# A hybrid encoder layer: the recurrent mixer's output products reordered, and 64-row passes padded with zero rows

## The chip, the cores and the metric

The kernel runs on one core of one Trainium2 chip. The metric is the device time of one execution, in microseconds (us), as the median of three runs. Engines are called by their names in the profile: PE (TensorE, matrix products; PEld is its loading of weights), DVE (VectorE), ACT (ScalarE), POOL (GpSimd) and SP (which issues DMAs). A matrix product writes to PSUM, which the other engines then read.

## What is computed

One layer over 1024 frames of width 1024: a half-step feed-forward network (FFN) with layer norm, a mixer, and a second half-step FFN. The mixer projects the frames once and feeds two branches, a recurrent one with 8 heads of 64 (RWKV-7) and a latent attention; both are gated, summed and projected.

```python
def layer(h):
    h = layer_norm(ALPHA * h + 0.5 * swiglu(h, ffn1_w1, ffn1_w3, ffn1_w2), ln1_g, ln1_b)
    proj = h @ w_in
    p_shift, p_mla, gate_logits = split(proj)
    y_rwkv = rwkv7_mixer(p_shift, ...) @ w_up_rwkv
    y_mla = mla_mixer(p_mla, ...) @ w_up_mla
    mix = (g_rwkv * y_rwkv + g_mla * y_mla) @ w_o
    h = layer_norm(ALPHA * h + mix, ln2_g, ln2_b)
    return layer_norm(ALPHA * h + 0.5 * swiglu(h, ffn2_w1, ffn2_w3, ffn2_w2), ln3_g, ln3_b)

def rwkv7_mixer(...):          # per head: a 64 x 64 state that every frame decays and updates
    w = -softplus(-(w0 + tanh(wd) @ w_decay_up)) - 0.5
    a = sigmoid(a0 + ad @ w_iclr_up)
    state = state * w_t + sa * b_t + v_t * k_t      # scan over the frames
    y_t = state @ r_t
```

## The kernel before, in words

**Precision.** A float32 operand is split into a rounded part (`hi`) and the rest (`lo`), and a product is three matrix passes, hi·hi, hi·lo and lo·hi (`mm3`, lines 273 to 275). The last FFN tile is only 64 wide: `ffn_stage1` puts its `hi` into rows 0 to 63 of `gh` and its `lo` into rows 64 to 127 (lines 325 to 327), against weights that the host stacked twice. So one pass over 128 rows gives hi·hi and lo·hi (line 356), and a second pass over rows 0 to 63 alone gives hi·lo (line 357). `lora_za` (lines 587 and 588), the two low-rank products with inner width 64 (for `w0` and `a0`), works in the same manner.

**FFN.** `block` runs over groups of tiles of the hidden width. Each of the two FFNs has one group (the last, tiles 18 to 21) that holds the 64-wide tile: for 8 row tiles and 2 halves it issues three `mm3` and the pair of lines 356 and 357, 11 matmuls in all. `load_w` brings a weight tile in: a DMA, the rounding on ACT (line 218) and the rest on POOL (line 219).

**Mixer.** PE's order is written out by hand here (`mid` turns the scheduler off for PE alone). The recurrent branch is four tasks of two heads each (`rwkv_task`). Between its steps a task yields a number, and `drive` fills PE for about so many microseconds with other work: jobs of `Fill`, mostly `dense` projections of three 128-row matmuls a step. Each job's weights are loaded up to two jobs ahead. At the end of a task, a chain over 16 chunks of 64 frames gives the states `sa` (lines 870 to 876), and the output products follow (lines 878 to 888): for each head `hd` of the pair and each chunk c a product with `m` and `qv` (128 rows, line 884), and for c > 0 one with `rr` and the state (the 64 rows of that head, line 887), which is added to the first. Chunk c writes PSUM rows 0 to 63 or 64 to 127 after its parity. A task thus issues 62 products, and each is two instructions in the trace: 124. One head fills one PSUM tile of the pool `pr`, which has three, and ACT copies each out to `y` (line 888). Then DVE, ACT and POOL normalize `y` (lines 894 to 902), while PE does 11 us of filling (`GAP["gn"]`), and PE transposes the result (line 909). Behind the mark "gn" the next task's features begin; behind the fourth task the attention's first loads do.

The tile scheduler sets the order on DVE, ACT, POOL and SP, and PE's outside the mixer.

Of the kernel before, what the change touches and what calls it, by code (L numbers as in the profile page):

```python
# [9 lines left out]
F32 = mybir.dt.float32  # L10
F32R = mybir.dt.float32r
AF = mybir.ActivationFunctionType
ALU = mybir.AluOpType
# [3 lines left out]
P = 128  # L17
# [4 lines left out]
HALF = 512  # L22
D_FF = 2752
NF = D_FF // P
# [3 lines left out]
NCH = S // CH  # L28
# [179 lines left out]
    return K.wsp if K.wsp2 is None or K.wn % 2 else K.wsp2  # L208


def load_w(K, src, n=1024, rows=P):
    nc = K.nc
    raw = K.wraw.tile([P, 1024], F32, name="raw")
    (nc.gpsimd if K.pq else nc.sync).dma_start(out=raw[:rows, :n], in_=src)
    pool = w_pool(K)
    hi = pool.tile([P, 1024], F32R, name="wh", tag="w")
    lo = pool.tile([P, 1024], F32R, name="wl", tag="w")
    nc.scalar.copy(out=hi[:rows, :n], in_=raw[:rows, :n])  # L218
    nc.gpsimd.tensor_tensor(out=lo[:rows, :n], in0=raw[:rows, :n], in1=hi[:rows, :n].bitcast(F32), op=ALU.subtract)  # L219
    return hi, lo  # L220

# [109 lines left out]
def block(K, stage1, w2, groups, ln, resid, emit_h, last=False):  # L331
    nc = K.nc
    accs = [None] * NT
    hT = None
    for gi, fs in enumerate(groups):
        gs = [stage1(f) for f in fs]
        first, final = gi == 0, gi == len(groups) - 1
        ws = [load_w(K, w2[f]) for f in fs]
        if final:
            gb = ln_begin(K, ln)  # L340
        for t in range(NT):
            tsl = slice(t * P, (t + 1) * P)
            if first:
                accs[t] = K.acc.tile([P, D], F32, name="acc", tag="acc")
                r = K.tmp.tile([P, D], F32, name="r", tag="r", bufs=2)
                nc.sync.dma_start(out=r, in_=resid(t))
            for n, ns in halves():
                ps = K.py.tile([P, HALF], F32, name="y", tag="y")
                for q in range(len(fs)):
                    gh, gl = gs[q]  # L350
                    wh, wl = ws[q]
                    st, sp = q == 0, q == len(fs) - 1
                    if gl is not None:
                        mm3(nc, ps, gh[:, tsl], gl[:, tsl], wh[:, ns], wl[:, ns], st, sp)
                    else:
                        nc.tensor.matmul(ps, lhsT=gh[:, tsl], rhs=wh[:, ns], start=st, stop=False)
                        nc.tensor.matmul(ps, lhsT=gh[0:64, tsl], rhs=wl[0:64, ns], start=False, stop=sp)
                if first:
                    nc.vector.scalar_tensor_tensor(out=accs[t][:, ns], in0=r[:, ns], scalar=ALPHA, in1=ps,  # L359
                                                   op0=ALU.mult, op1=ALU.add)  # L360
                elif final:
                    if n == 0:
                        su = K.small.tile([P, 2], F32, name="su")
                    nc.vector.scalar_tensor_tensor(out=accs[t][:, ns], in0=accs[t][:, ns], scalar=1.0, in1=ps,
                                                   op0=ALU.mult, op1=ALU.add, accum_out=su[:, n:n + 1])
                else:
                    nc.vector.tensor_tensor(out=accs[t][:, ns], in0=accs[t][:, ns], in1=ps, op=ALU.add)  # L367
            if final:
                hT = ln_tile(K, t, accs[t], su, gb, hT, emit_h, transpose=not last)
    return hT  # L370
# [183 lines left out]
def prt(K, name="pr"):  # L554
    return K.pr.tile([P, HALF], F32, name=name, tag="pr")


def load_w2(K, src, n=HALF, rows=P):
    nc = K.nc
    raw = K.wraw.tile([P, 1024], F32, name="raw")  # L560
    (nc.gpsimd if K.pq else nc.sync).dma_start(out=raw[:rows, :n], in_=src)
    w = w_pool(K).tile([P, 2, HALF], F32R, name="w2", tag="w")
    nc.scalar.copy(out=w[:rows, 0, :n], in_=raw[:rows, :n])
    nc.gpsimd.tensor_tensor(out=w[:rows, 1, :n], in0=raw[:rows, :n], in1=w[:rows, 0, :n].bitcast(F32), op=ALU.subtract)
    return w


# [9 lines left out]
            return  # L577


def lora_za(K, x, n, rows, bias, w):  # L580
    nc = K.nc
    for i in range(NRT):
        csl = slice(i * P, (i + 1) * P)
        o = K.d.tile([P, S], F32, name="lo", tag="d")
        for h, hs in halves():
            ps = prt(K)
            nc.tensor.matmul(ps, lhsT=w[:, 0, csl], rhs=x[:, hs], start=True, stop=False)
            nc.tensor.matmul(ps, lhsT=w[rows, 1, csl], rhs=x[rows, hs], start=False, stop=True)
            nc.scalar.activation(out=o[:, hs], in_=ps, func=AF.Sigmoid, bias=vec(K, bias, i))
            yield 0.43  # L590
        nc.sync.dma_start(out=K.lod[i, n], in_=o)
# [95 lines left out]
def rwkv_task(K, i, r, k, v, store):  # L687
    nc = K.nc
    yield from rwkv_features(K, i, r, k, v)
    ar, bk, yb, wl = K.feat  # L690
    yield GAP["bk"]
    hd_ = lambda h: slice(h * 64, h * 64 + 64)

    bkt, qv, pq = [], [], []
    for h in range(2):
        bt = rt(K, "bkt", [P, 8, P])
        for b in range(2):
            ps = prt(K)
            for q in range(4):
                c = 4 * b + q  # L700
                nc.tensor.transpose(out=ps[:, q * P:(q + 1) * P],
                                    in_=bk[h][:, c // 2, 2 * (c % 2):2 * (c % 2) + 2, :].rearrange("p s x -> p (s x)"),
# [3 lines left out]
    ma = []  # L706
    for g in range(4):
        m = rt(K, "ma", [P, 2, 2, 2, P])
        for hd in range(2):
            ps = prt(K)  # L710
            for q in range(4):
                c = 4 * g + q
                h, cl = c // 8, c % 8
                nc.tensor.matmul(ps[:, q * P:(q + 1) * P],
                                 lhsT=bk[h][hd_(hd), cl // 2, 2 * (q % 2):2 * (q % 2) + 2, :].rearrange("p s x -> p (s x)"),
                                 rhs=ar[h][hd_(hd), :, cl * CH:(cl + 1) * CH], start=True, stop=True)
            nc.vector.tensor_tensor(out=m[:, :, hd], in0=ps.rearrange("p (a e x) -> p a e x", e=2, x=P),
                                    in1=K.mask.rearrange("p (o q x) -> p o q x", o=1, q=1).broadcast_to([P, 2, 2, P]),
                                    op=ALU.mult)
        ma.append(m)  # L720
    dl = K.dram.tile([64, 32, 32], F32, name=f"dl{i}")
    for g in range(4):
        for e in range(2):
            for b in range(2):
                ln0 = (e * 2 + b) * 16 + g * 4
                src = ma[g][64 * e + 32 * b:64 * e + 32 * b + 32, :, :, e, 32 * b:32 * b + 32]
# [29 lines left out]
    for h, hs in halves():  # L756
        qt = rt(K, "qv", [P, 8, P])
        ps = prt(K)
        for q in range(4):
            c = h * HALF + q * P  # L760
# [96 lines left out]
    for h in range(2):  # L857
        ps = prt(K)
        n = 8 - h
# [10 lines left out]
    for c in range(1, NCH - 1):  # L870
        ps = K.pst.tile([P, CH], F32, name="st", tag="st")
        yield GAP["c0" if c == 1 else "chain"]
        for hd in range(2):
            nc.tensor.matmul(ps[hd_(hd)], lhsT=gg[hd_(hd), c, :], rhs=state(c)[hd_(hd)], start=True, stop=True)
        nc.vector.scalar_tensor_tensor(out=sa[:, c + 1, :], in0=ps, scalar=wl[:, c:c + 1], in1=sl[:, c, :],
                                       op0=ALU.mult, op1=ALU.add)
    yield GAP["chain"]
    for hd in range(2):
        ps = prt(K)
        for c in range(NCH):  # L880
            p, e = c // 2, c % 2
            m = ma[p // 2][:, p % 2]
            o = slice(p * 64, p * 64 + 64)
            nc.tensor.matmul(ps[hd_(e), o], lhsT=m[:, hd, e, 64:128], rhs=qv[c // 8][:, c % 8, hd_(hd)],  # L884
                             start=True, stop=c == 0)
            if c > 0:
                nc.tensor.matmul(ps[hd_(e), o], lhsT=rr[hd_(hd), c, :], rhs=state(c)[hd_(hd)], start=False, stop=True)  # L887
        nc.scalar.copy(out=y[:, :, hd_(hd)], in_=ps.rearrange("p (a x) -> p a x", x=64))

    y3 = y.rearrange("p t (h x) -> p (t h) x", x=64)  # L890
    mu = K.rsm.tile([P, 16], F32, name="mu", tag="mu")
# [88 lines left out]
def mid_body(K, h1T):  # L980
# [109 lines left out]
        fill.add([lambda: load_w(K, a["w_in"][idx])] + srcs, gen)  # L1090

    def lora1(n, x, rows, bias):
        return [lambda: load_w2(K, a["w_lora"][n])], lambda w: lora_za(K, T[x], n, rows, bias, w)

    def first(w0, w1):
        pss = [K.pd.tile([P, S], F32, name="pd", tag="pd") for _ in range(2)]
# [425 lines left out]
```

## Time and profile before

| | |
|---|---|
| runs | 2587.5, 2590.99 and 2593.37 us; median 2590.99 |
| profiled execution | span 2588.0 us from the first to the last instruction; no other time of it is listed |
| busy, share of the span | PE 96%, PEld 78%, DVE 41%, ACT 26%, POOL 28% |
| mean granted TensorE clock | 0.968 of full speed |
| HBM traffic | 87 GB/s over the span |

A row of a timeline gives the start and the duration of an instruction, its engine, its line, and the tiles as output<-inputs; a bracket at its end says how long the engine had been idle and what ended that. Matmuls overlap: the time from one start to the next is what a stream costs, not the duration. In a row of windows, "(x64)" counts instructions, and the clock (PEclk, 1.00 is full speed) and the DMA engines' busy share stand behind the five engines.

### The profile page before, as it was taken

The numbers are of one execution on the slowest core, as the hardware profiler recorded it, in microseconds if no ns is written. First come the engines' busy times: TensorE is split into PE (matmuls) and PEld (weight loads), VectorE is DVE, ScalarE is ACT, GpSimd is POOL, SyncE is SP. The second block draws the span as 40 slices with busy tenths as digits, with TensorE's granted clock in tenths as the row PEclk, the third lists the DMA queues.
The fourth block names the chain that finished last, engine by engine and source line by source line (L and its number), as shares of the span: only waits on it lengthen the run. The fifth ranks groups of instructions, "written<-read, shape, count | busy, mean of one in ns | idle before, by whom it ended". The sixth has DMA issues, their size and how long they took to land.

```text
span 2588.0 us, 31920 instructions
## 1 busy us (share of the span) xinstructions
PE 2495.6 (96%) x13138; PEld 2024.5 (78%) x13138; DVE 1059.7 (41%) x1751; ACT 670.0 (26%) x1055; POOL 720.9 (28%) x506
## 2 busy tenths in 40 slices
PE   9999999999999899998999979889999999999998
PEld 7888888888767777777777668767788888888886
DVE  4222222222344525526245456775622222222225
ACT  3111111111353223111122256652511111111111
POOL 4222222222344114123131333343512222222220
PEclk9999999999999989989989889999999999999999
DMA  5211111111123322212324555454232111111111
GB/s 203 90 49 50 49 49 46 46 48 49 55 98 133 85 91 71 69 66 90 99 82 125 201 184 141 151 207 175 106 106 66 49 49 49 49 49 49 49 41 65
DMA packets 91681, 228.42 MB, mean 88 GB/s; under 512 B 34760, under 2 KB 35144, under 8 KB 91536
## 3 DMA queue, kind: packets, MB, share of 16 engines
q1 hardware_dynamic: 84672, 202.21, 23.7%
q0 software_dynamic: 6864, 24.19, 2.9%
q8 instruction: 103, 1.69, 0.3%
q14 instruction: 42, 0.34, 0.0%
HBM read 168.29 MB, written 58.06 MB: 87 GB/s over the span
## 4 chain that ended last, share of the span: by engine, by line
PE 44%; DVE 4%; DMA 2%; issue 1%; ACT 1%; POOL 1%; SPq 0%; POOLq 0%; DVEq 0%; ACTq 0%
PE h L273 6%; PE h L274 6%; PE h L275 6%; PE y L273 4%; PE y L274 4%; PE y L275 4%; PE pd L273 2%; PE pd L275 2%; PE pd L274 2%; PE s L273 1%; PE s L274 1%; PE s L275 1%; PE pr L1401 1%; PE pr L887 1%; PE pr L884 1%
## 5 line engine op out<-in xcount | busy, mean ns | idle before, releaser
L219 POOL TENSOR_TENSOR wl<-raw,wh 128x1024 fp32r<-128x1024 f32 x172 | 415.7, 2423 | 1363.4 <-ACT wh L218 1151.3
L274 PE MATMUL h<-xl,wh 128*128 128x512 f32 x1376 | 536.2, 390 | 1.8 <-DVE xl L263 1.8
L275 PE MATMUL h<-xh,wl 128*128 128x512 f32 x1376 | 535.7, 390 | 0.0
L273 PE MATMUL h<-xh,wh 128*128 128x512 f32 x1376 | 533.2, 390 | 2.1 <-DVE xh L262 2.1
L218 ACT CAST wh<-raw 128x1024 fp32r<-128x1024 f32 x172 | 178.8, 1052 | 857.9 <-issue 311.4
L367 DVE TENSOR_TENSOR acc<-acc,y 128x512 f32<-128x512 f32 x272 | 184.8, 684 | 419.5 <-PE y L275 419.5
L273 PE MATMUL y<-wh,gh 128*128 128x512 f32 x800 | 317.1, 396 | 8.9 <-DVE acc L359 4.0
L275 PE MATMUL y<-wh,gl 128*128 128x512 f32 x800 | 312.9, 392 | 3.6 <-DVE gl L925 3.6
L274 PE MATMUL y<-wl,gh 128*128 128x512 f32 x800 | 312.8, 391 | 0.0
L274 PEld LDWEIGHTS h<-xl,wh 128*128 128x128 f32 x1376 | 258.8, 188 | 56.6 <-DVE xl L263 2.9
L273 PEld LDWEIGHTS h<-xh,wh 128*128 128x128 f32 x1376 | 258.3, 188 | 55.8 <-issue 2.2
L275 PEld LDWEIGHTS h<-xh,wl 128*128 128x128 f32 x1376 | 258.7, 188 | 53.6
L273 PE MATMUL pd<-xh,wh 128*128 128x512 f32 x576 | 244.0, 424 | 23.4 <-DVE mu_v L545 11.6
L274 PE MATMUL pd<-xl,wh 128*128 128x512 f32 x576 | 231.3, 402 | 0.2 <-DVE xl L925 0.2
L275 PE MATMUL pd<-xh,wl 128*128 128x512 f32 x576 | 231.1, 401 | 0.0
L319 DVE SCALAR_TENSOR_TENSOR g<-h,s 128x512 f32<-128x512 f32 x84 | 58.1, 692 | 409.7 <-PE h L275 409.7
L273 PEld LDWEIGHTS y<-wh,gh 128*128 128x128 f32 x800 | 151.2, 189 | 48.3 <-DVE acc L359 5.1
L275 PEld LDWEIGHTS y<-wh,gl 128*128 128x128 f32 x800 | 150.8, 189 | 36.0 <-DVE gl L925 4.5
L274 PEld LDWEIGHTS y<-wl,gh 128*128 128x128 f32 x800 | 151.2, 189 | 29.9
L273 PEld LDWEIGHTS pd<-xh,wh 128*128 128x128 f32 x576 | 112.1, 195 | 55.7 <-DVE mu_v L545 12.4
L925 DVE TENSOR_TENSOR gl<-g,gh 128x512 fp32r<-128x512 f32 (+1 forms) x85 | 119.7, 1408 | 47.4 <-ACT gh L923 47.2
L275 PEld LDWEIGHTS pd<-xh,wl 128*128 128x128 f32 x576 | 111.8, 194 | 25.2
(315 smaller groups left out, 3044.6 us busy)
## 6 DMA issues: line engine op xcount, KB each, us to landing
raw<-in_ffn_w_dram SPq DMA_DIRECT2D x128, 512.0 KB
raw<-in_w_in_dram POOLq DMA_DIRECT2D x36, 512.0 KB, 3.8
h<-acc SPq DMA_DIRECT2D x16, 512.0 KB
gates<-dt SPq DMA_DIRECT2D x16, 512.0 KB
xg<-gates SPq DMA_DIRECT2D x16, 512.0 KB
r<-h SPq DMA_DIRECT2D x16, 512.0 KB
lod<-lo SPq DMA_DIRECT2D x12, 512.0 KB
latn<-lw SPq DMA_DIRECT2D x10, 512.0 KB
```

Of the source, the lines that this page charges most:

```text
L218: nc.scalar.copy(out=hi[:rows, :n], in_=raw[:rows, :n])
L219: nc.gpsimd.tensor_tensor(out=lo[:rows, :n], in0=raw[:rows, :n], in1=hi[:rows, :n].bitcast(F32), op=ALU.subtract)
L273: nc.tensor.matmul(out, lhsT=lh, rhs=rh, start=start, stop=False)
L274: nc.tensor.matmul(out, lhsT=lh, rhs=rl, start=False, stop=False)
L275: nc.tensor.matmul(out, lhsT=ll, rhs=rh, start=False, stop=stop)
L319: nc.vector.scalar_tensor_tensor(out=g, in0=p3, scalar=0.5, in1=s, op0=ALU.mult, op1=ALU.mult)
L367: nc.vector.tensor_tensor(out=accs[t][:, ns], in0=accs[t][:, ns], in1=ps, op=ALU.add)
L884: nc.tensor.matmul(ps[hd_(e), o], lhsT=m[:, hd, e, 64:128], rhs=qv[c // 8][:, c % 8, hd_(hd)], start=True, stop=c == 0)
L887: nc.tensor.matmul(ps[hd_(e), o], lhsT=rr[hd_(hd), c, :], rhs=state(c)[hd_(hd)], start=False, stop=True)
L925: nc.vector.tensor_tensor(out=lo, in0=src, in1=hi.bitcast(F32), op=ALU.subtract)
L1401: nc.tensor.transpose(out=tp[:, q * P:(q + 1) * P], in_=pt2[q % 2][:, j * P:(j + 1) * P], identity=K.ident)
```

## The change

It has two parts. In `rwkv_task` both heads' PSUM tiles are taken at once (`pys`); first come all 32 products with `m`, then all 30 with `rr`, the heads alternating. `start` is set only for the first chunk pair. Both copies to `y` stand behind all products. In the FFN and in `lora_za`, the second pass runs over all 128 rows: `load_w` and `load_w2` write zeros into the half of the low weights that the pass didn't use (a memset on POOL) and subtract on the other 64 rows only.

```diff
--- before.py
+++ after.py
@@ -208,7 +208,7 @@
     return K.wsp if K.wsp2 is None or K.wn % 2 else K.wsp2
 
 
-def load_w(K, src, n=1024, rows=P):
+def load_w(K, src, n=1024, rows=P, zero=None):
     nc = K.nc
     raw = K.wraw.tile([P, 1024], F32, name="raw")
     (nc.gpsimd if K.pq else nc.sync).dma_start(out=raw[:rows, :n], in_=src)
@@ -216,6 +216,9 @@
     hi = pool.tile([P, 1024], F32R, name="wh", tag="w")
     lo = pool.tile([P, 1024], F32R, name="wl", tag="w")
     nc.scalar.copy(out=hi[:rows, :n], in_=raw[:rows, :n])
+    if zero is not None:
+        nc.gpsimd.memset(lo[zero].bitcast(F32), 0.0)
+        rows = P - (zero.stop - zero.start)
     nc.gpsimd.tensor_tensor(out=lo[:rows, :n], in0=raw[:rows, :n], in1=hi[:rows, :n].bitcast(F32), op=ALU.subtract)
     return hi, lo
 
@@ -335,7 +338,7 @@
     for gi, fs in enumerate(groups):
         gs = [stage1(f) for f in fs]
         first, final = gi == 0, gi == len(groups) - 1
-        ws = [load_w(K, w2[f]) for f in fs]
+        ws = [load_w(K, w2[f], zero=slice(64, P) if f == NF else None) for f in fs]
         if final:
             gb = ln_begin(K, ln)
         for t in range(NT):
@@ -354,7 +357,7 @@
                         mm3(nc, ps, gh[:, tsl], gl[:, tsl], wh[:, ns], wl[:, ns], st, sp)
                     else:
                         nc.tensor.matmul(ps, lhsT=gh[:, tsl], rhs=wh[:, ns], start=st, stop=False)
-                        nc.tensor.matmul(ps, lhsT=gh[0:64, tsl], rhs=wl[0:64, ns], start=False, stop=sp)
+                        nc.tensor.matmul(ps, lhsT=gh[:, tsl], rhs=wl[:, ns], start=False, stop=sp)
                 if first:
                     nc.vector.scalar_tensor_tensor(out=accs[t][:, ns], in0=r[:, ns], scalar=ALPHA, in1=ps,
                                                    op0=ALU.mult, op1=ALU.add)
@@ -555,13 +558,16 @@
     return K.pr.tile([P, HALF], F32, name=name, tag="pr")
 
 
-def load_w2(K, src, n=HALF, rows=P):
+def load_w2(K, src, n=HALF, rows=P, lo=None):
     nc = K.nc
     raw = K.wraw.tile([P, 1024], F32, name="raw")
     (nc.gpsimd if K.pq else nc.sync).dma_start(out=raw[:rows, :n], in_=src)
     w = w_pool(K).tile([P, 2, HALF], F32R, name="w2", tag="w")
     nc.scalar.copy(out=w[:rows, 0, :n], in_=raw[:rows, :n])
-    nc.gpsimd.tensor_tensor(out=w[:rows, 1, :n], in0=raw[:rows, :n], in1=w[:rows, 0, :n].bitcast(F32), op=ALU.subtract)
+    ls = lo or slice(0, rows)
+    if lo is not None:
+        nc.gpsimd.memset(w[64 - lo.start:P - lo.start, 1, :n].bitcast(F32), 0.0)
+    nc.gpsimd.tensor_tensor(out=w[ls, 1, :n], in0=raw[ls, :n], in1=w[ls, 0, :n].bitcast(F32), op=ALU.subtract)
     return w
 
 
@@ -577,7 +583,7 @@
             return
 
 
-def lora_za(K, x, n, rows, bias, w):
+def lora_za(K, x, n, bias, w):
     nc = K.nc
     for i in range(NRT):
         csl = slice(i * P, (i + 1) * P)
@@ -585,7 +591,7 @@
         for h, hs in halves():
             ps = prt(K)
             nc.tensor.matmul(ps, lhsT=w[:, 0, csl], rhs=x[:, hs], start=True, stop=False)
-            nc.tensor.matmul(ps, lhsT=w[rows, 1, csl], rhs=x[rows, hs], start=False, stop=True)
+            nc.tensor.matmul(ps, lhsT=w[:, 1, csl], rhs=x[:, hs], start=False, stop=True)
             nc.scalar.activation(out=o[:, hs], in_=ps, func=AF.Sigmoid, bias=vec(K, bias, i))
             yield 0.43
         nc.sync.dma_start(out=K.lod[i, n], in_=o)
@@ -875,17 +881,25 @@
         nc.vector.scalar_tensor_tensor(out=sa[:, c + 1, :], in0=ps, scalar=wl[:, c:c + 1], in1=sl[:, c, :],
                                        op0=ALU.mult, op1=ALU.add)
     yield GAP["chain"]
+    pys = [prt(K) for _ in range(2)]
+    osl = lambda p: slice(p * 64, p * 64 + 64)
+    for p in range(8):
+        m = ma[p // 2][:, p % 2]
+        for hd in range(2):
+            for e in range(2):
+                c = 2 * p + e
+                nc.tensor.matmul(pys[hd][hd_(e), osl(p)], lhsT=m[:, hd, e, 64:128], rhs=qv[c // 8][:, c % 8, hd_(hd)],
+                                 start=p == 0, stop=False)
+    for p in range(8):
+        for e in range(2):
+            c = 2 * p + e
+            if c == 0:
+                continue
+            for hd in range(2):
+                nc.tensor.matmul(pys[hd][hd_(e), osl(p)], lhsT=rr[hd_(hd), c, :], rhs=state(c)[hd_(hd)],
+                                 start=False, stop=p == 7)
     for hd in range(2):
-        ps = prt(K)
-        for c in range(NCH):
-            p, e = c // 2, c % 2
-            m = ma[p // 2][:, p % 2]
-            o = slice(p * 64, p * 64 + 64)
-            nc.tensor.matmul(ps[hd_(e), o], lhsT=m[:, hd, e, 64:128], rhs=qv[c // 8][:, c % 8, hd_(hd)],
-                             start=True, stop=c == 0)
-            if c > 0:
-                nc.tensor.matmul(ps[hd_(e), o], lhsT=rr[hd_(hd), c, :], rhs=state(c)[hd_(hd)], start=False, stop=True)
-        nc.scalar.copy(out=y[:, :, hd_(hd)], in_=ps.rearrange("p (a x) -> p a x", x=64))
+        nc.scalar.copy(out=y[:, :, hd_(hd)], in_=pys[hd].rearrange("p (a x) -> p a x", x=64))
 
     y3 = y.rearrange("p t (h x) -> p (t h) x", x=64)
     mu = K.rsm.tile([P, 16], F32, name="mu", tag="mu")
@@ -1090,7 +1104,7 @@
         fill.add([lambda: load_w(K, a["w_in"][idx])] + srcs, gen)
 
     def lora1(n, x, rows, bias):
-        return [lambda: load_w2(K, a["w_lora"][n])], lambda w: lora_za(K, T[x], n, rows, bias, w)
+        return [lambda: load_w2(K, a["w_lora"][n], lo=rows)], lambda w: lora_za(K, T[x], n, bias, w)
 
     def first(w0, w1):
         pss = [K.pd.tile([P, S], F32, name="pd", tag="pd") for _ in range(2)]
```

On PE, the end of a task's chain and its output products (`pr<-qv,ma` are those with `m`, `pr<-sl,rr` and `pr<-sa,rr` those with `rr`; `pd` are dense matmuls of the filling). Before, the first seven products of 62:

```order
L275 MATMUL pd<-xh,wl 128x512
L884 MATMUL pr<-qv,ma 64x64 x2
L887 MATMUL pr<-sl,rr 64x64
L884 MATMUL pr<-qv,ma 64x64
L887 MATMUL pr<-sa,rr 64x64
L884 MATMUL pr<-qv,ma 64x64
L887 MATMUL pr<-sa,rr 64x64
```

Now, all 62 and the dense matmul behind them:

```order
L278 MATMUL pd<-xh,wl 128x512
L891 MATMUL pr<-qv,ma 64x64 x32
L899 MATMUL pr<-sl,rr 64x64 x2
L899 MATMUL pr<-sa,rr 64x64 x28
L276 MATMUL pd<-xh,wh 128x512
```

The 62 products of a task now stand in two runs; what stands ahead and behind is the same.

On DVE, behind the fourth task's products (`mu`, `y` and `vr` are the normalization of `y`, `ku` the key projection of the filling). Before:

```order
L894 TENSOR_REDUCE mu<-y 128x16
L1202 TENSOR_TENSOR ku<-pd,kbc 128x512
L895 TENSOR_SCALAR mu<-mu 128x16
L896 TENSOR_TENSOR y<-y,mu 128x1024
L1202 TENSOR_TENSOR ku<-pd,kbc 128x512
```

Now:

```order
L908 TENSOR_REDUCE mu<-y 128x16
L1216 TENSOR_TENSOR ku<-pd,kbc 128x512
L909 TENSOR_SCALAR mu<-mu 128x16
L1216 TENSOR_TENSOR ku<-pd,kbc 128x512
L910 TENSOR_TENSOR y<-y,mu 128x1024
```

The second product of the key projection has moved ahead of the subtraction on `y`.

## Rows read from the trace of the kernel before

**Rows 1.** The page, part 1: busy us (share of the span) by engine.

```profile
PE 2495.6 (96%) x13138; PEld 2024.5 (78%) x13138; DVE 1059.7 (41%) x1751; ACT 670.0 (26%) x1055; POOL 720.9 (28%) x506
```

**Rows 2.** PE's waits, whole span: for what, us in total, times, longest.

```profile
PE pd L273 <- DVE mu_v L545: 11.6, 2, 5.8
```

**Rows 3.** Windows, four output stretches: PE, PEld, DVE, ACT, POOL busy, PEclk, DMA, GB/s.

```profile
952.54:974.12 21.58, 21.58 (x125) 15.44 (x125) 0.24 (x2) 2.56 (x3) 3.93 (x3) 0.61 0.29 103
...
1122.04:1142.93 20.89, 20.89 (x126) 14.95 (x125) 0.00 (x0) 0.58 (x1) 0.00 (x0) 0.64 0.00 1
...
1289.22:1310.06 20.84, 20.84 (x125) 14.95 (x125) 0.00 (x0) 0.58 (x1) 0.00 (x0) 0.64 0.08 32
...
1451.95:1474.11 22.16, 22.16 (x125) 15.83 (x124) 5.13 (x5) 3.19 (x5) 6.91 (x4) 0.58 0.43 159
```

**Rows 4.** PE's timeline, first stretch: start us, duration us, instruction.

```profile
952.55 0.34 PE L884 MATMUL pr<-qv,ma 128*64 128x64 f32 x4
...
952.81 0.32 PE L887 MATMUL pr<-sl,rr 64*64 64x64 f32 x2
...
953.07 0.33 PE L884 MATMUL pr<-qv,ma 128*64 128x64 f32 x2
```

**Rows 5.** PE's timeline and window, a run of 188 small instructions.

```profile
1088.51 1.73 PE L840 MATMUL pr<-ma,pt 64*64 64x64 f32 x58
...
1091.87 1.97 PE L862 MATMUL pr<-qv,bkt 128*64 128x64 f32 x60
...
1093.77 0.50 PE L273 MATMUL pd<-xh,wh 128*128 128x512 f32 x1
...
1088.51:1093.77 5.26, 5.26 (x190) 5.12 (x189) 3.59 (x7) 0.00 (x0) 0.00 (x0) 1.00 0.03 6
```

**Rows 6.** PE's timeline, lines 779 and 781: first and last of 32 instructions.

```profile
850.33 0.27 PE L779 MATMUL pr<-qv,ma 64*64 64x64 f32 x1 [0.52 <-DVE qv L764]
...
851.26 0.22 PE L781 MATMUL pr<-qv,ma 64*64 64x64 f32 x1
```

**Rows 7.** PE's timeline, dense matmuls behind the second stretch: first and 14th.

```profile
1142.93 0.79 PE L273 MATMUL pd<-xh,wh 128*128 128x512 f32 x1
...
1148.49 0.39 PE L274 MATMUL pd<-xl,wh 128*128 128x512 f32 x1
```

**Rows 8.** Timeline of PE and weight loads (PEld), first FFN's last group.

```profile
675.65 0.39 PE L273 MATMUL y<-wh,gh 128*128 128x512 f32 x1
...
677.47 0.19 PEld L356 LDWEIGHTS y<-wh,gh 128*128 128x128 f32 x1
...
677.70 0.39 PE L356 MATMUL y<-wh,gh 128*128 128x512 f32 x1
...
678.01 0.18 PEld L357 LDWEIGHTS y<-wl,gh 64*128 64x128 f32 x1 [0.35 <-issue]
...
678.44 0.50 PE L273 MATMUL y<-wh,gh 128*128 128x512 f32 x1
...
680.59 0.39 PE L356 MATMUL y<-wh,gh 128*128 128x512 f32 x1
```

**Rows 9.** PE's timeline, low-rank product: two successive passes of line 587.

```profile
761.44 0.39 PE L587 MATMUL pr<-x,w 128*128 128x512 f32 x1
...
763.68 0.39 PE L587 MATMUL pr<-x,w 128*128 128x512 f32 x1
```

**Rows 10.** Line 732, a GpSimd memset: ns min/median/max, first and last start.

```profile
L732 POOL MEMSET lt<- x4: 944/970/972, 843.4 to 1353.6; 64x1024 f32 x4
```

**Rows 11.** Timeline behind the third stretch: last normalization step, then its transposes.

```profile
1322.28 1.21 DVE L902 TENSOR_TENSOR y<-y,vr 128x1024 f32<-128x1024 f32 x1
...
1324.33 1.03 PE L909 MATMUL pr<-ident,y 128*128 128x128 f32 x8
```

**Rows 12.** VectorE's timeline behind the fourth stretch: subtraction and the product behind it.

```profile
1477.88 2.26 DVE L896 TENSOR_TENSOR y<-y,mu 128x1024 f32<-128x1024 f32 x1
...
1480.06 0.68 DVE L1202 TENSOR_TENSOR ku<-pd,kbc 128x512 f32<-128x512 f32 x1
```


## The prediction, made before the changed kernel was run

> **What bounds the kernel now.** I read the engines' busy time first, then what PE waits for, then the stretches in which PE is busy without doing much. PE is busy 96% of the span and no other engine above 41%, weight loads apart [rows 1]; its longest wait by a chain of the mixer is 11.6 us [rows 2]. So time can hardly be won by ending waits, only by making PE's own stream shorter. The windows over the four tasks' output products show where it is long: 21.58, 20.89, 20.84 and 22.16 us, 85.47 us in all, at a mean clock of 0.58 to 0.64 [rows 3]. PE counts as busy throughout, yet each stretch holds only 124 small instructions. The timeline of the first shows why: the two 128-row instructions of a product and the two 64-row instructions of the next follow each other at 0.26 us a change [rows 4]. Elsewhere 188 instructions of the same sizes, in two long runs, take 5.26 us at a clock of 1.00, 0.028 us each [rows 5].
>
> **The output products.** The change leaves 124 instructions and takes away 58 of 59 changes of shape in each task. The first run (64 instructions, 128 rows by 64) has the form of line 862, which takes (1093.77 - 1091.87) / 60 = 0.032 us each with the change back to dense matmuls: 2.0 us. The second (60, 64 rows by 64) has the form of lines 840 and 851, (1091.87 - 1088.51) / 128 = 0.026 us: 1.6 us [rows 5]. Together 3.6 us, four times 14.4, so 85.47 - 14.4 = **71.1 us** go. Within the second run each product changes its row half, which lines 840 and 851 do not. Lines 779 and 781 alternate row halves at (851.26 - 850.33) / 31 = 0.030 us [rows 6], so I add nothing. The other end, a full change of 0.26 us at each of 30 products [rows 4], would cost 7.8 in place of 1.6 us, four times 6.2.
>
> **The clock.** Under the old stretches the granted clock falls to its lower level, 1.2 in place of 2.4 GHz, and the dense matmuls behind them begin there: 13 take 1148.49 - 1142.93 = 5.56 us [rows 7], where the full-speed pace of 2.05 / 9 = 0.228 us [rows 8] gives 3.0, that is 0.2 us lost for each. The four stretches leave 9, 13, 13 and 12 such matmuls, 9.4 us. The clock was 1.00 all through the run of 188 [rows 5], so the shorter new ones should not lower it. But not all comes back. PE meets the transposes of `y` behind a fixed amount of filling, and if that runs faster it waits for the normalization, whose start also moves back by one copy (0.58 us, ACT's whole work in the second and third window [rows 3]), since both now stand behind the last product. In the third task the normalization ends 1322.28 + 1.21 = 1323.49, and the transposes begin at 1324.33, 0.84 us later [rows 11]; in the other three the same two rows leave 4.0, 1.3 and 2.2 us. Less 0.6 each, these slacks let through 1.8, 0.7, 0.2 and 1.6, or 4.3 us; some ACT steps of these chains themselves wait for the dense matmuls and come earlier, so I take **5 us**, with 0 and 9.4 as ends.
>
> **The FFN's padded pass.** One round of 11 matmuls takes 680.59 - 677.70 = 2.89 us, where the pace gives 11 x 0.228 = 2.51; the idle 0.35 us ahead of the 64-row load shows where the rest sits [rows 8]. A 128-row pass among its like costs no more than the pace, so 0.38 us go, 32 times: **12.3 us**. PE waits for nothing there and the last round's tail (layer norm and store of one row tile) stays.
>
> **The low-rank products.** Here a round is 8 matmuls, 763.68 - 761.44 = 2.24 us against 8 x 0.228 = 1.82 [rows 9]: 0.42 us, 16 times, **6.7 us**. The low end is 0, if ACT's sigmoid behind each pass, or the stores, hold PE back.
>
> **What it adds.** Four memsets on POOL, two of 1024 and two of 512 elements a row; the nearest takes 0.97 us [rows 10]. POOL is busy 28% of the time [rows 1] and the weights are made ahead of their use, so I cost them at nothing; uncovered, 3.9 us. The fourth task's subtraction on `y` now stands behind the second product of the key projection. Before, that began at 1480.06, as soon as the 2.26 us of the subtraction from 1477.88 were done [rows 12]; at full clock PE delivers its input about 2 us earlier, ahead of the subtraction's turn. Nothing, at most its 0.68 us. Of work that lost its cover there is none on DVE in the first three windows (0.24, 0.00 and 0.00 us busy); the fourth has 0.43 x 22.16 = 9.5 us of DMA and 6.91 us of POOL under it [rows 3], which end later against PE now, up to 9.5 - 3.6 = 5.9 us.
>
> **The sum.** 71.1 + 5 + 12.3 + 6.7 = 95.1 us off the span of 2588.0 gives 2492.9. The runs' median, 2590.99, lies 3.0 above that span, which I keep: **2496 us**.
>
> **The rivals.**
>
> *The gain returns in part as waits.* The fourth window's DMA and POOL work [rows 3] holds up what the attention loads, 4 to 6 us, and the clock's 5 us are lost in waits on DVE, whose queue already stopped PE for 5.8 us at a time [rows 2]. Against it: three stretches hide no DVE work. It gives about 2506.
>
> *A change of row half is a change of shape.* Each `rr` product switches the half and both halves write the same columns, which lines 779 and 781 don't do. At 0.26 us each, 25 us are lost, 2521. [Rows 6] speak against it.
>
> *Row groups and loads.* In the trace, the 128-row load for line 356 begins at 677.47, 0.23 us ahead of its matmul at 677.70 and beside the one before it, which uses the same rows; the 64-row load stands 0.35 us idle [rows 8]. Were a load only to run beside a matmul on other rows, each of the 48 padded passes would show its 0.19 us load [rows 8], 9.1 us less gain: 2505. The Trainium skill ("TensorE: Matmul & The Clock Gate", Part 3, The mechanism) states such a rule: weight loads overlap running matmuls only where their row groups differ, which speaks for keeping half-height passes. The trace disagrees with it here, with the 0.23 us just named.
>
> *The pace is not the changes' doing.* If 0.26 us were what two such products cost, through adding to the columns just written, the stretches would stay at 85 us; only 12.3 + 6.7 = 19 us go, 2572. Against it: the FFN's dense matmuls add to the columns just written at 0.228 us for 512 columns [rows 8].
>
> *The whole gain is eaten*, by weights that come too late for a faster PE. It would take waits of 95 us where the longest group has 11.6 [rows 2]: 2591.
>
> *Slower, by the clock.* The narrow runs could bring the clock down as the old stretches did, and the dense filling behind them keep it there. At 0.2 us a matmul [rows 7] the 95 us are gone after 475 matmuls at the low level, 119 behind each stretch; the rows show 13 before it rises. With 140 each it would be about 2608.
>
> **How the numbers follow.** Chances: the forecast 0.73, waits 0.14, row halves 0.06, loads 0.02, not the changes 0.02, all eaten 0.01, slower 0.02. About 0.2% of the time, 5.2 us, is what a measurement of this kernel can tell from no change. Five cases are faster by more, 0.97; one the same, 0.01; one slower, 0.02. Low end: all of the clock's 9.4 us (4 more), runs at 0.026 us throughout (2 more), and 3 for the scatter of the runs: 2486. High end: 2506 of the waits, and 8 for a row half that costs in part and for scatter: 2514. The cases beyond it hold about 0.1.
>
> **What would show it.** Right: the four stretches, from the first output product to the next dense matmul, take 3.4 to 4 us each; the clock there and behind is 1.00; a round of the FFN's last group takes 2.5 us and one of the low-rank product 1.8; no idle stands ahead of the second pass. PE's waits for the transposes of `y` are new, below 2.5 us each. Wrong: a stretch above 6 us (then the row halves cost), a round still at 2.9 us (then the padding isn't the cure), or waits of PE in the mixer that grew by more than 10 us in sum.

## The result, and the profile after

The changed kernel takes 2498.24 us (median of four runs, 2496.97 to 2501.32); the kernel before, measured beside it, 2589.24 us (four runs, 2587.09 to 2593.37). The ratio is 0.9644, with a 95% interval of 0.9633 to 0.9655: 91 us less. The profiled execution's span is 2495.9 us after 2588.0, 92.1 us less, and that difference is accounted for below.

Busy time by engine, from the page of the changed kernel (us, share of the span, instructions):

```profile
PE 2394.7 (96%) x13138; PEld 1970.5 (79%) x13138; DVE 1059.1 (42%) x1751; ACT 668.7 (27%) x1055; POOL 728.8 (29%) x510
```

PE executes as many instructions as before [rows 1] and is busy 100.9 us less. None of its instructions was taken away; they take less time. The windows over the four output stretches, from the first output product to the next dense matmul (us, PE busy, PEclk, DMA share, GB/s):

```profile
938.50:941.59 3.09, 3.09 (x125) 1.00 0.84 268
1093.74:1096.83 3.09, 3.09 (x125) 1.00 0.00 0
1240.90:1243.99 3.09, 3.09 (x125) 1.00 0.51 198
1387.38:1390.48 3.10, 3.10 (x126) 1.00 0.96 342
```

These answer to [rows 3]: 85.47 us have become 12.37, and a granted clock of 0.58 to 0.64 has become 1.00 (2.4 GHz). PE's timeline of the first stretch, answering to [rows 4] and, in its last three rows, to [rows 7]:

```profile
938.50 2.08 PE L891 MATMUL pr<-qv,ma 128*64 128x64 f32 x64
940.52 0.27 PE L899 MATMUL pr<-sl,rr 64*64 64x64 f32 x2
...
940.64 1.03 PE L899 MATMUL pr<-sa,rr 64*64 64x64 f32 x54
941.59 0.50 PE L276 MATMUL pd<-xh,wh 128*128 128x512 f32 x1
941.93 0.40 PE L277 MATMUL pd<-xl,wh 128*128 128x512 f32 x1
942.16 0.40 PE L278 MATMUL pd<-xh,wl 128*128 128x512 f32 x1
```

The first run's 64 instructions start over 940.52 - 938.50 = 2.02 us, 0.032 us each. The second run's 60 take 941.59 - 940.52 = 1.07 us, 0.018 us each: faster than the small matmuls of [rows 5, 6]. The dense matmuls behind go at 0.23 us from the second on.

The padded passes, in PE's timeline: the FFN's round (to compare with [rows 8]) and the low-rank product's (with [rows 9]):

```profile
677.20 0.39 PE L359 MATMUL y<-wh,gh 128*128 128x512 f32 x1
677.43 0.39 PE L360 MATMUL y<-wl,gh 128*128 128x512 f32 x1
677.66 0.39 PE L276 MATMUL y<-wh,gh 128*128 128x512 f32 x1
...
679.70 0.39 PE L359 MATMUL y<-wh,gh 128*128 128x512 f32 x1
...
750.72 0.39 PE L593 MATMUL pr<-x,w 128*128 128x512 f32 x1
...
752.57 0.40 PE L593 MATMUL pr<-x,w 128*128 128x512 f32 x1
```

The FFN's round is 2.50 us (2.89 before), the low-rank round 1.85 us (2.24), and the second pass follows the first at the pace of a dense matmul.

PE's waits over the span, the four groups that grew most (us in total, times, longest), answering to [rows 2]:

```profile
PE pd L276 <- DVE mu_v L548: 13.7, 2, 7.9
...
PE pd L276 <- DVE ku L1216: 4.5, 4, 2.2
PE pr L655 <- POOL ns L647: 4.0, 2, 2.6
...
PE pr L923 <- DVE y L916: 2.2, 1, 2.2
```

Before, the same four groups had 11.6, 2.4, 2.5 and 0 us. All of PE's waits together rose from 82.5 to 91.1 us, 8.6 us more: that much of the gain came back as waiting.

### The profile page after: what moved, and what is told of

Same layout as the page of the kernel before. It is cut to its first block, busy times and chain, and to the rows that moved or that the text cites. A ratio compares the mean times of both kernels' runs of the same rounds, so it can differ in the third digit from the quotient of the medians.

```text
span 2495.9 us, 31937 instructions
## 1 busy us (share of the span) xinstructions
PE 2394.7 (96%) x13138; PEld 1970.5 (79%) x13138; DVE 1059.1 (42%) x1751; ACT 668.7 (27%) x1055; POOL 728.8 (29%) x510
## 4 chain that ended last, share of the span: by engine, by line
PE 42%; DVE 5%; issue 3%; DMA 3%; ACT 1%; POOL 1%; SPq 0%; DVEq 0%; POOLq 0%; ACTq 0%
PE h L277 6%; PE h L276 6%; PE h L278 6%; PE y L276 4%; PE y L277 4%; PE y L278 4%; PE pd L276 1%; PE pd L277 1%; PE pd L278 1%; PE s L276 1%; PE s L277 1%; PE s L278 1%; PE pr L1415 1%; DVE lt L748 1%; DVE tp L746 1%
## 5 line engine op out<-in xcount | busy, mean ns | idle before, releaser
L222 POOL TENSOR_TENSOR wl<-raw,wh 128x1024 fp32r<-128x1024 f32 (+1 forms) x172 | 416.6, 2428 | 1314.8 <-ACT wh L218 1105.0
```

## The experiments

Eight kernels, in two sets of four, each set beside the kernel before (2590.37 and 2591.36 us). Three of them were executed once; there the lengths of the stretches carry the reading, since the total of one execution scatters by some us.

### The new order alone, the padding alone

The first kernel is the one before with only the output products' two loops of the change (both banks, runs of one shape). The second is the changed kernel with these loops put back as they were, so that only the zero-filled passes remain.

> The output products in runs of one shape into two banks, without the filling of the 64-row passes. If the parts add up (the FFN's 32 rounds gave 0.39 us each and the 16 low-rank rounds 0.39 us each in the traces, together 18.7 us, none of it lost), the new order alone is worth what is left of the 92 us: about 73 us, 2516 us (2512 to 2520). If the earlier arrival from the low-rank passes is what the longer waits of the later tasks ate (6.8 us of waits more between 690 us and the end of the middle part), the order alone keeps these and gains about 80 us, 2509 us. If the clock alone had been at fault and not the changes of shape, this run and the whole change would not differ by the 18.7 us at all.

> The filling of the 64-row passes alone, with the output products in their former order. If the parts add up: 12.5 us from the FFN's rounds and 6.2 us from the low-rank rounds, 2570 us (2568 to 2573), and the four output stretches again 20.8 to 22.2 us with the granted clock at 0.58 to 0.64. If the low-rank part (off the narrow work's path) is eaten by waits: 12.5 us, 2577 us.

Measured: the order alone 2521.36 us, ratio 0.9732 (0.9719 to 0.9746), 69 us less; its four stretches are 3.09 to 3.10 us. The padding alone 2572.63 us, ratio 0.9925 (0.9912 to 0.9939), 18 us less; its four stretches are 21.57, 22.35, 20.94 and 20.69 us long. The parts add up within their intervals: 69 and 18 are 87, against 91 together; the order alone came out 1 us above the 2512 to 2520 us expected for that case. The 80 us that would follow if the padding's earlier arrival caused the waits are ruled out. Of PE's waits the order alone has 90.6 us, the whole change 91.1, the padding alone 86.2, and 82.5 before. The longer waits for `ns` and the new one for `y` come with the new order (4.0 and 2.2 us with the order alone; 2.5 and none with the padding alone). The longer wait for `mu_v` does not come with it alone: it is 13.0 us with the order alone, 13.4 with the padding alone, 11.6 before. Its cause stays open.

### Alternating shapes, but never on columns just written

This separates the change of shape from adding to columns that were written just before. The 64-row product follows 128-row products of other columns:

```diff
-    for p in range(8):
...
-    for p in range(8):
...
+    for k in range(8):
+        mprod(*ms[k])
+    for k in range(len(rs)):
+        rprod(*rs[k])
+        if k + 8 < len(ms):
+            mprod(*ms[k + 8])
```

> The output products go into two banks as in the changed kernel, but a 128-row and a 64-row product alternate, the 64-row one adding to columns that were written some sixteen products earlier. If a change of shape costs 0.26 us whatever columns are written: some 47 changes in each stretch make it 13 to 18 us instead of 3.1, the granted clock in them falls below 0.7, and the time is 2538 to 2558 us. If what cost was adding to columns just written: the stretches stay at 3 to 4 us and the time at 2498 to 2502 us.

Measured: 2558.71 us in one execution, with stretches of 17.5 to 18.3 us. The first stretch, PE's timeline and then its window (us, PE busy, PEclk, DMA share, GB/s):

```profile
941.60 0.69 PE L889 MATMUL pr<-qv,ma 128*64 128x64 f32 x16
942.22 0.33 PE L894 MATMUL pr<-sl,rr 64*64 64x64 f32 x2
942.47 0.33 PE L889 MATMUL pr<-qv,ma 128*64 128x64 f32 x2
942.73 0.33 PE L894 MATMUL pr<-sl,rr 64*64 64x64 f32 x2
...
958.49 0.47 PE L894 MATMUL pr<-sa,rr 64*64 64x64 f32 x2
958.89 0.47 PE L889 MATMUL pr<-qv,ma 128*64 128x64 f32 x2
959.29 0.69 PE L894 MATMUL pr<-sa,rr 64*64 64x64 f32 x12
...
941.60:959.91 18.31, 18.31 (x125) 0.63 0.36 122
```

As long as one shape runs, eight products take 0.62 us; from the first change on, each product takes 0.26 us at the full clock, and 0.40 us once the granted clock has fallen. That is the pace of [rows 4], with the accumulation taken out of it. The change of shape is the price, and the clock falls in this stretch too (0.63 in the mean).

Where the time goes shows in the weight loads of the kernel before, here the first load behind the first change of shape:

```profile
952.81 0.19 PEld L887 LDWEIGHTS pr<-sl,rr 64*64 64x64 f32 x2
```

It begins at 952.81, when its own matmul is shown to start [rows 4], while the dense load of [rows 8] begins 0.23 us ahead of its matmul. So at a change the load is not hidden. Whether the load is held up by itself, or everything waits until the matmuls of the other shape have left the engine, these traces do not separate.

### Fifteen changes instead of one

The runs are cut to one `p` each (four products of either shape, but two in the first 64-row run), so that a stretch has 15 changes.

> The output products into two banks as in the changed kernel, in runs of four, so that the shape changes 15 times in a stretch instead of once. If the price is a fixed one for each change at the full clock (0.26 us for a product behind a change instead of some 0.06 us, so 0.2 us more): 14 x 0.2 = 2.8 us more in each stretch, 5.9 us instead of 3.1, some 11 us in all, 2509 us, as long as the granted clock stays at 1.00. If the clock falls as it did in the former order: 4 to 6 us more in each stretch, 2514 to 2522 us. If the price is per product of the smaller shape and not per change: no more than the changed kernel, 2498 us.

Measured: 2507.50 us in one execution. PE's timeline and window of the first stretch:

```profile
942.80 0.45 PE L889 MATMUL pr<-qv,ma 128*64 128x64 f32 x8
943.18 0.34 PE L894 MATMUL pr<-sa,rr 64*64 64x64 f32 x8
943.46 0.45 PE L889 MATMUL pr<-qv,ma 128*64 128x64 f32 x8
...
942.15:947.39 5.24, 5.24 (x125) 1.00 0.91 299
```

The clock holds, and 14 more changes cost 5.24 - 3.09 = 2.15 us, 0.15 us each; 0.2 had been expected, from products that alternate one by one. So a change costs 0.15 to 0.2 us at the full clock. The FFN's lone 64-row pass, with a change ahead and one behind, agrees: filled up, it saves 0.39 us. The total, 9 us above the changed kernel, is near four times 2.15.

### The second run with the heads outside

```diff
...
-            for hd in range(2):
-                nc.tensor.matmul(pys[hd][hd_(e), osl(p)], ...
...
+    for hd in range(2):
+        for c in range(1, NCH):
+            p, e = c // 2, c % 2
+            nc.tensor.matmul(pys[hd][hd_(e), osl(p)], ...
...
```

> The second run (64-row products) with the heads in the outer loop: the row half of the operands and the bank stay the same for 15 products, then change once. If the 17.8 ns of an instruction come from two row halves working beside one another: 26 to 32 ns per instruction, the second run 1.6 to 1.9 us instead of 1.06, the whole some 2 to 3.5 us longer (2500 to 2502 us). If 17.8 ns is the price of a 64-row, 64-column product that waits for nothing: the second run stays at 1.06 us and the time at 2498 us.

Measured: 2502.94 us in one execution, and stretches of 3.84 to 3.85 us, 0.75 us longer each. From PE's timeline:

```profile
943.11 0.27 PE L896 MATMUL pr<-sl,rr 64*64 64x64 f32 x1
...
943.97 1.03 PE L896 MATMUL pr<-sa,rr 64*64 64x64 f32 x29
944.93 0.50 PE L276 MATMUL pd<-xh,wh 128*128 128x512 f32 x1
```

60 instructions in 1.82 us, 0.030 us each. So the 0.018 us is not the price of one small product: it comes when neighbours use different row halves and write different banks. Halves in turn that write one bank took 0.030 us too [rows 6], though there the output halves alternate as well. One row half with two banks in turn was not run. For 128-row products such banks gained nothing: the first run of the stretch, which changes its bank after every second product, takes 0.032 us an instruction, as the run into one bank does [rows 5].

### The same for the runs ahead of the chain

The two runs of 64-row products that make `rr` and `gg` (lines 846 and 857 after the change) are issued with the halves in turn into two banks:

```diff
-    for e in range(2):
-        ps = prt(K)
-        for p in range(8):
-            for hd in range(2):
+    pss = [prt(K) for _ in range(2)]
+    for p in range(8):
+        for hd in range(2):
+            for e in range(2):
...
```

> The changed kernel with the two runs of 64-row products ahead of the chain issued with the row halves in turn into two banks, as the output's second run is. If the 17.8 ns come from row halves in turn into two banks: 256 instructions for each task go from 26 ns to 17.8 ns, 64 us x 4 / 1000 x 8.2 ns, that is 1.0 us for each task, 4 us in all at most 8 (128 products of two instructions), 2490 to 2494 us, unless the copies behind them become a wait. If the 17.8 ns belong to the output's operands alone: no change, 2498 us.

Measured: 2497.29 us, ratio to the kernel before 0.9636 (0.9622 to 0.9650), which cannot be told from the changed kernel's 0.9644. PE's timeline says why:

```profile
901.28 1.16 PE L845 MATMUL pr<-ma,pt 64*64 64x64 f32 x64
902.26 0.28 PE L857 MATMUL pr<-bkt,pt 64*64 64x64 f32 x2
903.39 1.16 PE L857 MATMUL pr<-bkt,pt 64*64 64x64 f32 x62 [0.86 <-DVE rr L851]
904.48 1.97 PE L870 MATMUL pr<-qv,bkt 128*64 128x64 f32 x60
```

The runs take 0.98 us (64 instructions) and 1.09 us (62) instead of 1.7 (64 at 26 ns [rows 5]), so the gain holds for other operands as well. But the four banks that the two runs now want at once are not there: the pool has three, and PE waits 0.86 us in the first task, 3.4 us in the four, for VectorE to empty one. What is won goes there: from 901.28 to 904.48 the two runs together take 3.20 us, where they took 3.36 [rows 5].

### The chain as one product

Each chain step's two 64-row products become one 128-row product. Its weights need both heads' blocks on the diagonal and zeros elsewhere; the tile of the inverses (`tt`), which has this form already and is no longer needed then, holds them (`K.gd`). Memsets on POOL restore its zeros for the next task, and VectorE writes each head's block by itself (both left out here).

```diff
-    rr, gg = rt(K, "rr", [P, NCH, CH]), rt(K, "gg", [P, NCH, CH])
+    rr, gg = rt(K, "rr", [P, NCH, CH]), K.gd
...
-        for hd in range(2):
-            nc.tensor.matmul(ps[hd_(hd)], lhsT=gg[hd_(hd), c, :], rhs=state(c)[hd_(hd)], start=True, stop=True)
+        nc.tensor.matmul(ps, lhsT=gg[:, c, :], rhs=state(c), start=True, stop=True)
```

> The changed kernel with each chain step's two 64-row products made one 128-row product, whose weights hold both heads' blocks on the diagonal and zeros beside them. In the changed kernel's trace such a step holds dense work up by 0.35 us ahead of the next dense product and 0.10 us behind it. If a change of shape is the price wherever it stands, 56 steps go from 0.45 us to about 0.06 us (two more instructions of 26 to 32 ns) and the time falls by some 22 us, to 2476 us (2472 to 2482). If the steps' price is the small size of the products or the wait for the state, and not the shape: less than 4 us, 2494 us or more. The two heads' copies into the diagonal are four instead of two on VectorE, which may turn some 1.2 us for each task into waits.

Measured: **2481.88 us, ratio 0.9581 (0.9567 to 0.9594)**, beyond the changed kernel's interval: the best of all, 109 us under the kernel before and some 16 under the changed one. One chain step in PE's timeline of the changed kernel:

```profile
930.83 0.40 PE L278 MATMUL pd<-xh,wl 128*128 128x512 f32 x1
931.16 0.33 PE L880 MATMUL st<-sa,gg 64*64 64x64 f32 x4
931.42 0.50 PE L276 MATMUL pd<-xh,wh 128*128 128x512 f32 x1
931.76 0.40 PE L277 MATMUL pd<-xl,wh 128*128 128x512 f32 x1
```

and one with a single product:

```profile
909.44 0.39 PE L278 MATMUL pd<-xh,wl 128*128 128x512 f32 x1
909.67 0.33 PE L885 MATMUL st<-sa,tt 128*128 128x64 f32 x2
909.81 0.48 PE L276 MATMUL pd<-xh,wh 128*128 128x512 f32 x1
910.12 0.40 PE L277 MATMUL pd<-xl,wh 128*128 128x512 f32 x1
```

From the dense matmul ahead to the second behind, 0.93 us have become 0.68. Two dense matmuls at 0.23 are 0.46 of it, so the step costs 0.22 instead of 0.47 us. Over all 56 steps the mean falls from 0.91 to 0.68 us, which gives 13 of the 16 us; PE's waits, 88.7 instead of 91.1 us, fit most of the rest. The expected 22 was too much: the one product was reckoned at the pace of small products in a run (0.06 us), but alone between dense matmuls it holds the next up by 0.14 us and the one after it by 0.08.

### Both again

The chain as one product and the halves in turn, together.

> The chain steps as one product and the row halves in turn, together, on top of the change. If both gains hold and don't meet: about 22 plus 4 us under the changed kernel, 2472 us (2466 to 2480). If neither does: 2498 us.

Measured: 2489.67 us, ratio 0.9604 (0.9591 to 0.9617): 8 us slower than the chain's product alone. PE's waits are 100.0 us instead of 88.7, 11.3 more, among them the two that are new for lack of a bank:

```profile
PE pr L860 <- DVE rr L854: 3.4, 4, 0.9
...
PE pr L876 <- DVE tt L865: 2.0, 4, 0.5
```

The two runs gain nothing here: the first of these waits included, they take 3.20 us together in three tasks, where the chain's product alone has 3.36, but 3.78 instead of 3.36 in the first task, under a mean clock of 0.83. So the 8 us lie in the second new wait, 2.0 us, and in 5.9 us of longer waits of old groups (`mu_v` 14.7 instead of 12.4, for one). Why these grew is not shown. Three banks more evenly used were not tried.

## Why the prediction was right, and where its terms were off

It said 2496, the runs 2498; the span's gain was put at 95.1 us and is 92.1. (The forecast added 3.0 us from the span to the median; 2498.24 lies only 2.3 above the profiled span, so 0.7 of the 3.0 us that the span lacks is taken back.) The profile of before and of after, laid side by side at the same instructions, gives each term (the gain is the start before less the start after):

| term | forecast us | measured us | from |
|---|---|---|---|
| output products | 71.1 | 73.1 | windows of the stretches, 85.47 - 12.37 |
| clock behind them, less waits for `y` and `ku` | 5 | 4.1 | stretch to transposes: 20.1, 20.2, 18.0, 18.9 gained, 77.2 less 73.1 |
| FFN's padded pass | 12.3 | 12.2 | 6.1 in either FFN; a round is 0.39 us shorter |
| low-rank pass | 6.7 | 7.9 | 15 rounds of 0.39, and a first round of 1.97 instead of 3.88 us |
| everything else | 0 | -5.2 | see below |
| sum | 95.1 | 92.1 | |

**The output products.** The mechanism, a price for each change of shape and none for the products themselves, was right, and the stretch with alternating shapes at a distance shows it free of the accumulation. The stretches of 3.09 us lie below the 3.4 to 4 us that were named as the sign of it. Mis-sized was the second run: priced at 0.026 us an instruction, it takes 0.018, because the row halves in turn, which I costed at nothing and feared at 0.26 us, are a gain. That rival (a change of row half as a change of shape) has the wrong sign.

The Trainium skill ("TensorEngine Tiling (Array Packing)", Key Properties) says that changing the tiling mode, not just the tile, drains TensorE, and that different tiles work in parallel. Both are in keeping with these traces, which show no drain as such but add the sizes: 0.15 to 0.2 us for a change, and 0.018 against 0.030 us for two row halves with a bank each.

**The clock.** It was 1.00 in every new stretch and directly behind it; behind the fourth it fell again only after the last and longest of the waits for `ku` (2.23 us; 0.78 in the mean from there to the transposes). The dense matmuls behind the old stretches had lost 9 us, as counted, and the forecast let 5 through; 4.1 came. Where it was said to stop, it stopped, in PE's timeline behind the third stretch:

```profile
1258.04 1.06 PE L923 MATMUL pr<-ident,y 128*128 128x128 f32 x8 [2.19 <-DVE y L916]
```

This is the new wait for the transposes of `y` that was foreseen "below 2.5 us", in the task with the least slack [rows 11]. Behind the fourth stretch PE waits for `ku` three times more (0.96, 0.57 and 0.69 us), the place of [rows 12]; 2.2 us in all, where this had been costed at nothing, at most 0.68.

**The padding.** Right to 0.1 us in the FFN. In the low-rank product the first round, which follows a wait, was at the lower clock before (0.56) and is not after (1.00). That this term came out 1.2 us above the forecast is luck, as far as the runs show, and not the padding's doing: the order alone, which pads nothing, has this round at 2.73 us, and two padded kernels behind the same wait of 2.07 us have it at 1.96. The rival that loads hide only beside other rows is out: the loads of the padded passes begin while a matmul on the same 128 rows runs, as in the weight loads' timeline

```profile
677.21 0.19 PEld L360 LDWEIGHTS y<-wl,gh 128*128 128x128 f32 x1
```

0.22 us ahead of its matmul at 677.43, with line 359's running since 677.20, and the round has no 0.19 us to show for it. The Trainium skill's rule ("TensorE: Matmul & The Clock Gate", Part 3, The mechanism) that weight loads overlap running matmuls only where row groups differ therefore doesn't hold for these loads; the same section also lets a load into the background weight buffer run ahead, and that is in keeping with them. The memsets showed no price: 0.95 and 0.52 us each on POOL, and no new wait of PE on what they fill.

**The step that failed** is the one not in the sum: waits were counted only up to the transposes of `y`, and nothing for the tasks after. The second task gives back 5.8 us and the fourth 1.7. In the second, PE's first feature products come to `ns` earlier than POOL's power has it, and a dense matmul waits longer for `mu_v`:

```profile
967.46 0.91 PE L655 MATMUL pr<-ident,ns 128*64 128x128 f32 x6 [2.63 <-POOL ns L647]
...
1030.97 0.80 PE L276 MATMUL pd<-xh,wh 128*128 128x512 f32 x1 [7.91 <-DVE mu_v L548]
```

Before, the same two waits were 1.10 and 5.77 us. And a wait can cost more than its length: the window from line 655's first product to the products of `rk`, in the second task of the changed kernel,

```profile
967.46:978.26 10.80, 10.80 (x73) 0.86 0.31 112
```

and the same instructions in the kernel before (PE busy, PEclk, DMA share, GB/s):

```profile
1000.08:1009.39 9.31, 9.31 (x73) 1.00 0.37 131
```

73 instructions either way, but behind the longer wait the granted clock is 0.86 in the mean, and 1.49 us more are gone. 1.53 and 2.14 us of longer waits and this 1.49 make 5.2 of the 5.8 us; the other 0.6 goes in dense matmuls at the lower clock behind the wait for `mu_v`. In the fourth task the 1.7 us go in the products of `rk` and the dense matmul behind them, and there the wait ahead is 2.15 us in either kernel. The changed kernel, then the kernel before:

```profile
1277.48:1281.19 3.71, 3.71 (x6) 0.54 0.00 0
```

```profile
1343.74:1345.76 2.02, 2.02 (x5) 1.00 0.01 4
```

So the length of a wait does not settle whether the clock falls behind it. Of the ten kernels traced here, all with this wait at 2.14 to 2.15 us, four pass the place at 1.00 and six at 0.54 to 0.60; and the kernel with the rows in turn waits 2.52 us for `ns` and goes on at 1.00. What decides it stays open, and the 1.7 us are for that reason not a cost that could have been counted. The 3 us that other places gave on top (0.5 ahead of the first padded round, 2.5 in the attention and behind it) were not followed up.

The sum came out within 3 us in part by luck, because the errors have both signs: 2.0 and 1.2 us too little, 0.9, 0.1 and 5.2 too much.

## What to carry to other kernels

Where PE shows as fully busy over small matmuls, divide the stretch by the instructions and look at the shapes in turn: in this kernel products of different row counts cost 0.15 to 0.2 us at every change, in the mixer as in the FFN, and in the stretches with some 50 changes and more the clock fell for what follows, in those with 15 not. Issue them in runs of one shape, fill a lone half-height pass with zeros, or make it full height by a block diagonal; and give products of different row halves a bank each, if banks are free. When the busiest engine gets faster, count the waits of the tasks behind as well as of the one that was changed, and allow for a lower clock behind a wait.

## What the hardware showed that was not expected

Two 64-row products that use different row halves and write different banks go at 0.018 us an instruction (1.07 us for 60), where the same products take 0.030 with one half and one bank after the other (1.82 us). Both runs ahead of the chain showed the same with other operands (0.98 us for 64, 1.09 us for 62).

A single small product (two instructions) between dense matmuls costs 0.22 us, though its weights have the 128 by 128 shape of theirs and it streams 64 columns where they stream 512. Small products in a run take 0.06 us [rows 5]. As two products of half the height, with a change of row count ahead and behind, the same step costs 0.47. Why the single one costs so much is not shown.

The granted clock stayed at 1.00 in the stretch with 15 changes of shape (5.24 us), and fell within those of alternating shapes (17.5 to 22.2 us), though PE shows no idle time there: their first products go at 0.26 us each, their last at 0.40. The number of changes and the length of the stretch are not separated here.
